# A second buffer for the gate blocks of layer two, a first stage with one chain of norms and its modulation a tile ahead, and five buffers for the samples' states

## The chip, the cores and the metric

The kernel runs on one core of a Trainium2 chip. The metric is the time of one execution on the device in microseconds (µs), the median of several runs. The core's engines are named as in the profile: PE multiplies matrices (PEld is its loading of weights), DVE works on vectors, ACT computes activations and copies, POOL is GpSimd, and SP issues the transfers (DMA) in order. Every transfer named here is issued on SP.

## What is computed

One step of a decoder with two layers, for a prompt of 1024 tokens and 8 samples of 4 tokens each (32 rows). Each layer shifts and scales the normed input by values that come from a condition vector, runs a token mixer, and adds the gated result to its input:

```
def modulate(x, c, norm_g, w_mod, b_mod):
    shift, scale, gate = jnp.split(jax.nn.silu(c) @ w_mod + b_mod, 3, axis=-1)
    h = rms_norm(x, norm_g) * (1 + scale[:, None]) + shift[:, None]
    return h, gate[:, None]

x <- x + gate(c) * Branch(RMSNorm(x) * (1 + scale(c)) + shift(c))
```

The mixer of layer one is attention in a sliding window of 128 positions (16 query heads, 4 key and value heads, learned sinks). The mixer of layer two is a gated DeltaNet: 8 query and key heads, 16 value heads of 128, a short convolution, and one state of 128 x 128 for each value head. The samples bring their own states: 8 samples of 16 heads, 8 MB in fp32, read and written once. In both layers the input projection also gives a SiLU gate path `z`, which multiplies the mixer's output ahead of the output projection. The width of the model is 1024.

## The kernel before

**Precision.** A large projection is three matmuls on split operands: high part by high part, low by high and high by low (`hhi`, `hlo` for the activations; `wh`, `wl` for the weights). The split of a piece of weights is a cast on ACT (`wh`) and a subtraction on DVE or POOL (`wl`).

**Order.** The order of instructions is fixed when the program is built. The class `Core` keeps a clock for each engine and adds up an estimated duration for each instruction; jobs (generators) yield conditions such as `ready`, `idle` and `soon`, and the planner takes up the one whose condition holds. Nearly every instruction passes through its wrapper, so the profile gives it the line L84; one tells them apart by the names of their tiles. The compute engines keep this order. Transfers are put in an order of their own on SP when the program is built, as their buffers come free there; on the chip SP issues them one after the other, and an issue that waits holds up those behind it.

**The first stage** makes `hhi` and `hlo`, the modulated input, and computes the first two column blocks of the input projection at the same time.

- `turn_x` transposes nine pieces of `x` on PE, and DVE copies them to `zo`; ACT sums the squares (`xss`).
- `scale_x(n0, n1)` turns the sums into 1/rms (`rsx`) by a chain of 12 small operations on DVE. It is called for pieces 0 to 4 after the fifth `turn_x`, and for pieces 5 to 8 at the end.
- `spread_x(gi)` spreads `rsx` over the partitions by matmuls, and ACT copies the result to `rsb`, for three groups of columns. For the samples POOL then makes `fs`.
- `modulate(e)` multiplies the condition by the modulation's weights for feature tile `e` (16 small matmuls on `wm`), and ACT copies the result to `ma`. `fold(e, ma)` adds up its rows by two matmuls, and DVE makes the scale `Sc` and the shift `Sh`.
- `shape_h(k)` makes feature tile `k` of `hhi` and `hlo`: DVE computes `fu` from `zo`, `Sc` and `rsb`, ACT adds the shift and rounds (`hhi`), and DVE takes the rest (`hlo`). For the 32 sample rows, four small operations do the same on POOL.
- `first_part(k, p)` adds feature tile `k` to column block `p`: nine matmuls into three banks of PSUM (`pj`, `pj`, `tr` for block 0, `lg`, `lg`, `ob` for block 1).

The loop over the eight tiles has, in this order, `fold(k+1)`, `shape_h(k+1)`, both parts of `first_part(k)`, and `modulate(k+2)`. After it, `kproj(0)` and `qproj(0,0)` evacuate the six banks, and `qproj(0,1)` runs its projection (matmuls at L537) into the banks that the ring `pj3` gives (`pj`, `pj`, `tr`).

**Layer two.** Its chunks of the prompt go through projection, convolution, the solution of a triangular system (`X`, `Xd`, `UZ`) and the recurrence (`us`, `vo`, `S`). For each finished pair of chunks, `gating` normalises `vo` and multiplies it by the gate: the block `zl` (128 x 512, 256 KB) is loaded from `zd`, where the gate path was stored; ACT scales `vo`; PE transposes it into `ps_tr`; DVE multiplies into `zl`; and `zl` is stored in `gTd`, from where the output projection reads it (`of`):

```
zl = gp.tile([P, 2, 2 * P], F32, tag="zl", name="zl", bufs=ZB)
nc.sync.dma_start(zl, zd[rs_, ts_].rearrange("(h p) i -> p h i", p=P))
...
nc.vector.scalar_tensor_tensor(zf, pt, ong, zf, ALU.mult, ALU.mult)
give("tr", pt)
nc.sync.dma_start(gTd[rs_, ts_].rearrange("(h p) i -> p h i", p=P), zl)
```

There are 32 such blocks, and `zl` has `ZB` = 1 buffer.

**The samples' states.** From about 1400 µs on, `states_times` loads the states in 32 units of 256 KB (`S<-in_states`) into a ring of `SB` = 4 buffers. It multiplies them in pairs (`ps_lg<-S,zq`) and, after each pair, loads two more. The planner puts these matmuls between those of the output projection. Later `new_states` loads the states again, updates them and writes them.

Of the kernel before, what the change touches and what calls it, by code (L numbers as in the profile page):

```python
# [9 lines left out]
ALU = mybir.AluOpType  # L10
# [4 lines left out]
P = 128  # L15
# [171 lines left out]
def f(ap):  # L187
    return ap.bitcast(F32)
# [26 lines left out]
def body(tc, I, O, cst_ap, dbg=None):  # L215
# [10 lines left out]
    ps = tc.tile_pool(name="ps", bufs=1, space=PSUM)  # L226
    ps_guard, ps = ps, ps.__enter__()
    banks = {"pj": 2, "tr": 1, "mi": 2, "ob": 1, "lg": 2}
    rings = {"pj3": ("pj", "pj", "tr"), "ch": ("mi", "mi", "ob")}
    turns = dict.fromkeys(rings, 0)  # L230
    any_bank, pj_tag = "mi", "pj3"

    nkeep = COFF["wmask"][0]
    ZB, VB, SB = 1, 3, 4
    SP = (5, 21)
    AM = (6, 9)
    K = {'split': 4, 'add': 3, 'attend': 12, 'turning': 14, 'modulate': 31, 'cached': 9, 'wo': 39, 'turn': 0, 'ahead': 2, 'taps': 2, 'gating': 5, 'decay': 27, 'samples': 9, 'load': 4, 'mod': 9, 'shape': 9, 'decays': 8, 'prepare': 0, 'gather': 30, 'finish': 55, 'states': 21, 'core': 4, 'new': 9}
# [9 lines left out]
    SE = ("vector", "vector", "vector", "vector")  # L247
    LB_, SL = TB
    XB, FB = 14, 3

    def psb(tag=None):
        tag = tag or any_bank
        if tag in rings:
            turns[tag] += 1
            tag = rings[tag][(turns[tag] - 1) % len(rings[tag])]
        t = ps.tile([P, 512], F32, tag=tag, name="ps_" + tag, bufs=banks[tag])
        return nc.slot(tag, banks[tag], t) if isinstance(nc, Core) else t
# [161 lines left out]
    def split_w(raw, alloc=None):  # L419
        nk, ncol = raw.shape[1:]  # L420
        if alloc is None:
            hi = wq.tile([P, nk, ncol], F32R, tag="wh", name="wh", bufs=3)
            lo = wq.tile([P, nk, ncol], F32R, tag="wl", name="wl", bufs=3)
        else:
            hi, lo = alloc()
        last_split[:] = [nc.scalar.copy(hi, raw)]
        nc.gpsimd.tensor_sub(lo, raw, f(hi))
        return hi, lo
# [188 lines left out]
    def scale_x(n0, n1):  # L617

        sv = sm.tile([P, n1 - n0], F32, tag="sv4", name="sv4")
        nc.vector.tensor_scalar(sv, xss[:, n0:n1], 1.0 / D, EPS, ALU.mult, ALU.add)  # L620
        rsqrt(nc, sm, rsx[:, n0:n1], sv, n1 - n0, tag=f"rx{n0}")

    def spread_x(gi):

        a, b = GRP[gi]
        pb = psb(("lg", "ob", "lg")[gi])
        for t in range(3 * gi, 3 * gi + 3):
            parts, n = P if t < NB else TS, turns_x.index(t)
            nc.tensor.matmul(pb[:, t * P - a:t * P - a + parts], rsx[0:parts, n:n + 1].to_broadcast([parts, P]),
                             ident[0:parts, 0:parts], start=True, stop=True)  # L630
        nc.scalar.copy(rsb[:, a:b], pb[:, 0:b - a])
        if gi == 2:
            for i in range(2):
                nc.gpsimd.tensor_tensor(fs[:, 4 * i:4 * i + 4], zo[i][:, :, TP:T],
                                        rsb[:, TP:T].unsqueeze(1).to_broadcast([P, 4, TS]), ALU.mult)

    def modulate(e):

        pm = psb("mi")[:, 0:256]
        for k in range(KD):  # L640
            q = k % 4
            nc.tensor.matmul(pm[32 * q:32 * q + 32, :], cT[:, k, :], wms[e, k // 4][:, q, :], start=(k < 4), stop=(k >= 4),
                             skip_group_check=True)
        ma = xp.tile([P, 256], F32, tag="ma", name="ma", bufs=2)
        nc.scalar.copy(ma, pm)
        return ma

    def fold(e, ma):

        mT = psb("mi")  # L650
        for c in range(2):
            nc.tensor.matmul(mT[:, 32 * c:32 * c + 32], ma[:, c * P:(c + 1) * P], C["fold32"], start=True, stop=True)
        nc.vector.tensor_scalar(Sc[0][:, e, :], mT[:, 32:41], bS[:, e:e + 1], gT[:, 0, e:e + 1], ALU.add, ALU.mult)
        nc.vector.tensor_scalar(Sh[0][:, e, :], mT[:, 0:9], bT[:, e:e + 1], None, ALU.add)

    def shape_h(k):

        u = xp.tile([P, TP], F32, tag="fu", name="fu", bufs=FB)
        sc, sh = Sc[0][:, k, 0:1], Sh[0][:, k, 0:1]
        spans = [slice(0, GW), slice(GW, TP)]  # L660
        for cs in spans:
            nc.vector.scalar_tensor_tensor(u[:, cs], zo[k // 4][:, k % 4, cs], sc, rsb[:, cs], ALU.mult, ALU.mult)
            nc.scalar.activation(hhi[:, k, cs], u[:, cs], AF.Identity, bias=sh)
        for cs in spans:
            nc.vector.scalar_tensor_tensor(hlo[:, k, cs], u[:, cs], sh, f(hhi[:, k, cs]), ALU.add, ALU.subtract)
        bc, f4 = [P, DB, DS], fs[:, k, :].rearrange("p (b t) -> p b t", t=DS)
        nc.gpsimd.tensor_tensor(f4, f4, Sc[0][:, k, 1:9].unsqueeze(2).to_broadcast(bc), ALU.mult)
        nc.gpsimd.tensor_tensor(f4, f4, Sh[0][:, k, 1:9].unsqueeze(2).to_broadcast(bc), ALU.add)
        nc.gpsimd.tensor_copy(hhi[:, k, TP:T], fs[:, k, :])
        nc.gpsimd.tensor_sub(hlo[:, k, TP:T], fs[:, k, :], f(hhi[:, k, TP:T]))  # L670

    fps, fraws, fws = [], {}, {}

    def first_load(q):
        fraws[q] = wp.tile([P, 4, P], F32, tag="wr", name="wr", bufs=4)
        queued(fraws[q], I["win01"][q])

    def first_part(k, p_):

        hi, lo = fws[k // 2]  # L680
        for gi, (a, b) in enumerate(GRP):
            for n, (x, y) in enumerate(((hi, hhi), (hi, hlo), (lo, hhi))):
                nc.tensor.matmul(fps[p_][gi], x[:, 2 * p_ + k % 2, :], y[:, k, a:b], start=(k == 0 and n == 0),
                                 stop=(k == KD - 1 and n == 2))
# [4 lines left out]
    for n, t in enumerate(turns_x):  # L689
        turn_x(n, t)  # L690
        if n == 1:
            modulation_rows()
        if n == 4:
            scale_x(0, 5)
    queued(cst[:, early:], cst_ap[:, early:nkeep])
    wmod_load(2)
    first_load(1)
    spread_x(0)
    scale_x(5, 9)
    ma = modulate(0)  # L700
    fws[0] = split_w(fraws.pop(0))
    spread_x(1)
    spread_x(2)
    fold(0, ma)
    shape_h(0)
    ma = modulate(1)
    fps += [[psb(tag)[:, 0:b - a] for (a, b), tag in zip(GRP, tags)] for tags in (("pj", "pj", "tr"), ("lg", "lg", "ob"))]
    wmod_load(3)
    for k in range(KD):
        if k + 1 < KD:  # L710
            fold(k + 1, ma)
            shape_h(k + 1)
        first_part(k, 0)
        if k % 2 == 0 and k + 2 < KD:
            fws[k // 2 + 1] = split_w(fraws.pop(k // 2 + 1))
        first_part(k, 1)
        if k + 2 < KD:
            ma = modulate(k + 2)
        if k + 4 < KD:
            wmod_load(k + 4)  # L720
            if k % 2 == 0:
                first_load(k // 2 + 2)
    raws = []
    for q in range(2):
        raws.append(wp.tile([P, 4, P], F32, tag="wr", name="wr", bufs=4))
# [15 lines left out]
    if True:  # L741
# [107 lines left out]
        spare_ = []  # L849

        def qproj(pr, g):
            qs = []

            def evac(gi, a0, b0, pj):
                if gi == 0 and pr == 0 and g > 1:

                    if g == 2:
                        spare_.append(zp.tile([P, 4, T], F32R, tag="zo1", name="zq"))
                    qs.extend(spare_[0][:, 2 * (g % 2) + a, :] for a in range(2))
                elif gi == 0:  # L860
                    for a in range(2):
                        m = 4 * pr + 2 * (g % 4) + a if pr else 2 * g + a
                        if m > 4:
                            until(lambda: begun[0] >= NB * (1 if m < 9 else 3))
                        qs.append(at.tile([P, T], F32R, tag="qs", name="qs", bufs=5))
                for a in range(2):
                    own = slice(64 * a, 64 * a + 64)
                    oth = slice(64 - 64 * a, 128 - 64 * a)
                    nc.scalar.activation(qs[a][own, a0:b0], pj[own], AF.Copy, scale=0.125)
                    nc.vector.scalar_tensor_tensor(qs[a][oth, a0:b0], pj[own], 0.125, f(qs[a][own, a0:b0]),  # L870
                                                   ALU.mult, ALU.subtract)
                    if gi == 2:
                        src = pj[own, 1024 - a0:1056 - a0].rearrange("p (b r t) -> p b r t", r=2, t=DS)
                        for r in range(2):
                            c0 = 48 * r + 4 * g
                            nc.scalar.activation(qz[:, 2 * pr + a, :, c0:c0 + 4], src[:, :, r, :], AF.Copy, scale=0.125)

            if pr == 0 and g == 0:
                for gi, (a, b) in enumerate(GRP):
                    with tc.issue_after(last_split[0].ins):  # L880
                        evac(gi, a, b, fps[1][gi])
            elif pr == 0 and g == 1:
                project(None, None, P, hhi, hlo, evac, wq01)
            else:
                projected(evac)
            return qs
# [1826 lines left out]
```

## Time and profile before

| what | value |
|---|---|
| median of the runs | 1701.39 µs (1697.44 to 1703.25) |
| profiled execution | 1698.41 µs |
| its span | 1696.6 µs |
| busy share of the span | PE 94%, PEld 84%, DVE 72%, ACT 50%, POOL 14% |
| read and written in HBM | 147.54 MB and 49.84 MB |

The span runs from the first to the last recorded instruction. All places in the trace are given as µs from its start. The column PEclk of the windows is the granted clock of PE as a share of its full rate. A timeline row gives the start, the duration, the engine, the instruction as out<-in, and in brackets the idle time of the engine ahead of it and what ended it.

### The profile page before, as it was taken

What the parts mean: (1) busy time and instruction counts of PE and PEld (TensorE: products, weight loads), DVE (VectorE), ACT (ScalarE), POOL (GpSimd) and SP (SyncE); (2) the same over time, 40 slices, a digit from 0 to 9 for tenths busy, and PEclk for the clock granted to TensorE, in tenths of its full rate; (3) what the DMA queues carried; (4) which work ended last, traced back from release to release, by engine and by line L of the source; (5) the groups of instructions that cost most, each with busy time, mean ns of one, the idle gap of its engine ahead of it and who ended that gap; (6) DMA issues with size and microseconds to landing.
All of it is one profiled execution on the core that took longest, in us unless ns stands there. A gap on an engine that the chain in (4) does not pass through costs nothing.

```text
span 1696.6 us, 30465 instructions
## 1 busy us (share of the span) xinstructions
PE 1602.7 (94%) x10544; PEld 1419.6 (84%) x10544; DVE 1218.4 (72%) x3797; ACT 845.1 (50%) x2414; POOL 237.6 (14%) x321
## 2 busy tenths in 40 slices
PE   7899999999999999989999899999999998888897
PEld 6798888988678999879999898999999986556675
DVE  5626677566665687878988788887888867267677
ACT  4526565444334664546654654646655654233332
POOL 2400000002222001020011101001010032132332
PEclk8999999999999999989999999999999999998999
DMA  9332211125242323133313224232242156773785
GB/s 347 108 128 93 75 53 51 57 60 155 86 146 91 119 61 101 52 85 89 116 51 99 78 69 116 67 106 77 67 126 58 54 174 177 225 230 112 249 262 168
DMA packets 190890, 196.79 MB, mean 116 GB/s; under 512 B 86432, under 2 KB 137472, under 8 KB 190688
## 3 DMA queue, kind: packets, MB, share of 16 engines
q1 hardware_dynamic: 190736, 194.84, 37.4%
q8 instruction: 83, 1.36, 0.3%
q14 instruction: 71, 0.58, 0.1%
HBM read 147.54 MB, written 49.84 MB: 116 GB/s over the span
## 4 chain that ended last, share of the span: by engine, by line
PE 43%; DVE 9%; DMA 9%; ACT 3%; issue 2%; SPq 1%; POOL 0%; POOLq 0%; DVEq 0%; ACTq 0%
PE ps_pj L84 27%; PE ps_lg L84 6%; PE ps_mi L84 5%; PE ps_ob L84 2%; PE ps_tr L84 2%; DMA gTd<-zl 2%; DMA S<-in_states 1%; DMA zl<-zd 1%; DMA of<-gTd 1%; DMA out_new_s_s<-S 1%; DVE zl L84 1%; DMA wr<-in_gdn_w_out 1%; DMA out_y_p<-xt 1%; DVE S L84 1%; DVE rst L84 1%
## 5 line engine op out<-in xcount | busy, mean ns | idle before, releaser
L84 PE MATMUL ps_pj<-h2lo,wh 128*128 128x384 f32 (+1 forms) x1128 | 380.4, 337 | 0.0
L84 PE MATMUL ps_pj<-h2hi,wl 128*128 128x384 f32 (+1 forms) x1128 | 378.9, 336 | 0.9 <-DVE wl L84 0.9
L84 PE MATMUL ps_pj<-h2hi,wh 128*128 128x384 f32 (+1 forms) x1128 | 379.4, 336 | 0.0
L84 PEld LDWEIGHTS ps_pj<-h2hi,wl 128*128 128x128 f32 x1128 | 213.9, 190 | 4.2 <-DVE wl L84 1.3
L84 PEld LDWEIGHTS ps_pj<-h2hi,wh 128*128 128x128 f32 x1128 | 214.2, 190 | 2.9
L84 PEld LDWEIGHTS ps_pj<-h2lo,wh 128*128 128x128 f32 x1128 | 214.0, 190 | 2.8
L84 POOL TENSOR_TENSOR Xd<-Xc,cst 32x128 f32<-32x128 f32 x128 | 68.5, 535 | 435.0 <-DMA Xc<-Xdd 251.5
L84 PE MATMUL ps_pj<-hlo,wh 128*128 128x384 f32 (+1 forms) x376 | 124.7, 332 | 0.0
L84 PE MATMUL ps_pj<-hhi,wh 128*128 128x384 f32 (+1 forms) x376 | 124.7, 332 | 0.0
L84 PE MATMUL ps_pj<-hhi,wl 128*128 128x384 f32 (+1 forms) x376 | 123.6, 329 | 0.0
L84 POOL TENSOR_TENSOR xt<-xt,y 128x512 f32<-128x512 f32 (+1 forms) x48 | 65.4, 1364 | 219.3 <-DVE y L84 186.4
L84 DVE TENSOR_TENSOR wl<-wr,wh 128x512 fp32r<-128x512 f32 x120 | 83.3, 694 | 15.5 <-ACT wh L84 15.1
L84 DVE SCALAR_TENSOR_TENSOR vT<-XR,cT,vT 128x384 f32<-128x384 f32 (+1 forms) x144 | 80.8, 572 | 9.9 <-ACT vT L84 9.2
L84 ACT CAST wh<-wr 128x512 fp32r<-128x512 f32 x128 | 78.6, 616 | 16.9 <-PE ps_pj L84 15.2
L84 PEld LDWEIGHTS ps_pj<-hlo,wh 128*128 128x128 f32 x376 | 71.0, 189 | 10.6 <-issue 10.2
L84 PEld LDWEIGHTS ps_pj<-hhi,wh 128*128 128x128 f32 x376 | 71.0, 189 | 4.0 <-issue 3.8
L84 PEld LDWEIGHTS ps_pj<-hhi,wl 128*128 128x128 f32 x376 | 71.0, 189 | 2.8 <-issue 2.7
L84 ACT ACTIVATE qe<-ps_mi,Eg 128x128 f32<-128x128 f32 x112 | 34.9, 363 | 70.8 <-PE ps_mi L84 68.9
L84 DVE TENSOR_TENSOR X<-X,tmp 128x126 f32<-128x126 f32 (+22 forms) x248 | 63.8, 257 | 8.5
L84 ACT COPY XR<-ps_pj 128x384 f32<-128x384 f32 (+1 forms) x96 | 43.3, 451 | 52.6 <-PE ps_pj L84 52.4
L84 DVE TENSOR_TENSOR tmp<-X 128x126 f32<-128x126 f32 (+22 forms) x248 | 62.3, 251 | 7.3 <-POOL X L84 3.4
L84 ACT ACTIVATE prob<-prob,nm 128x256 f32<-128x256 f32 (+1 forms) x128 | 62.2, 488 | 9.6 <-DVE nm L84 9.4
(540 smaller groups left out, 3933.9 us busy)
## 6 DMA issues: line engine op xcount, KB each, us to landing
wr<-in_gwb SPq DMA_DIRECT2D x96, 256.0 KB
S<-in_states SPq DMA_DIRECT2D x40, 256.0 KB
xt<-in_x_prompt SPq DMA_DIRECT2D x16, 512.0 KB
wm<-in_wm SPq DMA_DIRECT2D x16, 512.0 KB
wr<-in_winb SPq DMA_DIRECT2D x32, 256.0 KB
wmod<-in_w_mod SPq DMA_DIRECT2D x32, 256.0 KB
wm<-in_w_mod SPq DMA_DIRECT2D x32, 256.0 KB
DP<-gcr SPq DMA_DIRECT2D x64, 128.0 KB
```

Of the source, the lines that this page charges most:

```text
L84: inst = fn(*args, **kwargs)
```

## The change

It has three parts.

1. `ZB` goes from 1 to 2 (the ring of `zl`), and `SB` from 4 to 5 (the ring of the samples' states).
2. The first stage is put in another order. There is one call `scale_x(0, 9)` after all pieces of `x`; `modulate(0)` stands ahead of it, `modulate(1)` and `fold(0)` behind it and ahead of the three `spread_x`; `fold(1)` follows `shape_h(0)`. In the loop, `modulate(k+2)` stands between the two parts of `first_part(k)`. The samples' four operations of `shape_h` move from POOL to DVE (three) and ACT (one). `hold(n)` issues `n` matmuls whose result nobody reads: one ahead of the `spread_x` and three behind `fold(1)`. With `LATEP` False, the last three parts keep their old order.
3. A ring `next` = (`mi`, `mi`, `pj`) gives the banks for the projection in `qproj(0,1)`.

```
-    rings = {"pj3": ("pj", "pj", "tr"), "ch": ("mi", "mi", "ob")}
+    rings = {"pj3": ("pj", "pj", "tr"), "next": ("mi", "mi", "pj"), "ch": ("mi", "mi", "ob")}
...
-    ZB, VB, SB = 1, 3, 4
+    ZB, VB, SB = 2, 3, 5
...
+    FH, LATEP = (1, 3), False
...
+        bc, f4 = [P, DB, DS], fs[:, k, :].rearrange("p (b t) -> p b t", t=DS)
+        nc.vector.tensor_tensor(f4, f4, Sc[0][:, k, 1:9].unsqueeze(2).to_broadcast(bc), ALU.mult)
+        nc.vector.tensor_tensor(f4, f4, Sh[0][:, k, 1:9].unsqueeze(2).to_broadcast(bc), ALU.add)
+        nc.scalar.copy(hhi[:, k, TP:T], fs[:, k, :])
         for cs in spans:
             nc.vector.scalar_tensor_tensor(hlo[:, k, cs], u[:, cs], sh, f(hhi[:, k, cs]), ALU.add, ALU.subtract)
-        bc, f4 = [P, DB, DS], fs[:, k, :].rearrange("p (b t) -> p b t", t=DS)
-        nc.gpsimd.tensor_tensor(f4, f4, Sc[0][:, k, 1:9].unsqueeze(2).to_broadcast(bc), ALU.mult)
-        nc.gpsimd.tensor_tensor(f4, f4, Sh[0][:, k, 1:9].unsqueeze(2).to_broadcast(bc), ALU.add)
-        nc.gpsimd.tensor_copy(hhi[:, k, TP:T], fs[:, k, :])
-        nc.gpsimd.tensor_sub(hlo[:, k, TP:T], fs[:, k, :], f(hhi[:, k, TP:T]))
+        nc.vector.tensor_sub(hlo[:, k, TP:T], fs[:, k, :], f(hhi[:, k, TP:T]))
+
+    def hold(n):
+
+        pt = psb("mi")
+        for _ in range(n):
+            nc.tensor.matmul(pt[:, 0:384], ident, zo[0][:, 0, 0:384], start=True, stop=True)
...
-        if n == 4:
-            scale_x(0, 5)
...
-    spread_x(0)
-    scale_x(5, 9)
     ma = modulate(0)
+    scale_x(0, 9)
+    ma1 = modulate(1)
+    fold(0, ma)
     fws[0] = split_w(fraws.pop(0))
-    spread_x(1)
-    spread_x(2)
-    fold(0, ma)
+    hold(FH[0])
+    for gi in range(3):
+        spread_x(gi)
     shape_h(0)
-    ma = modulate(1)
+    fold(1, ma1)
+    hold(FH[1])
...
         if k + 1 < KD:
-            fold(k + 1, ma)
+            if k:
+                fold(k + 1, ma)
             shape_h(k + 1)
-        first_part(k, 0)
+        if k < KD - 1:
+            first_part(k, 0)
         if k % 2 == 0 and k + 2 < KD:
             fws[k // 2 + 1] = split_w(fraws.pop(k // 2 + 1))
-        first_part(k, 1)
         if k + 2 < KD:
             ma = modulate(k + 2)
+        if k < KD - 2:
+            first_part(k, 1)
...
+    for k, p_ in ((KD - 1, 0), (KD - 2, 1), (KD - 1, 1)) if LATEP else ((KD - 2, 1), (KD - 1, 0), (KD - 1, 1)):
+        first_part(k, p_)
...
             elif pr == 0 and g == 1:
+                pj_tag = "next"
                 project(None, None, P, hhi, hlo, evac, wq01)
+                pj_tag = "pj3"
```

Apart from the first stage, the compute engines keep the order of their instructions up to about 1420 µs. Behind that the planner puts the matmuls on `S` at other places among those of the output projection.

More of the change, by code (lines that the diff above doesn't have):

```diff
@@ L851, in qproj @@
         def qproj(pr, g):
+            nonlocal pj_tag
             qs = []
```

## The prediction

> **What bounds the kernel now.** I read the page first, then the waits, then the windows over stretches that differ, and the timelines of the stretches that stood out. Ahead of all, the page's parts 1, 2 and 4:
>
> ```profile
> span 1696.6 us, 30465 instructions
> PE 1602.7 (94%) x10544; PEld 1419.6 (84%) x10544; DVE 1218.4 (72%) x3797; ACT 845.1 (50%) x2414; POOL 237.6 (14%) x321
> ...
> PE 43%; DVE 9%; DMA 9%; ACT 3%; issue 2%; SPq 1%; POOL 0%; POOLq 0%; DVEq 0%; ACTq 0%
> ```
>
> PE is the bound: 94 µs of the span are without PE work, and no edit here removes a product of weights. So a gain can only be PE's idle time and the stretches in which its clock is half. The waits (engine, tile, releaser: total µs, times, longest) say which idle time the change touches:
>
> ```profile
> DVE zl L84 <- DMA zl<-zd: 25.2, 11, 7.4
> PE ps_tr L84 <- DVE zl L84: 9.7, 6, 4.3
> PEld ps_mi L84 <- ACT ma L84: 8.3, 7, 2.2
> PE ps_lg L84 <- DMA S<-in_states: 8.2, 5, 3.3
> ```
>
> Three places follow: the first stage (`ma`), the gate blocks (`zl`) and the samples' states (`S`). The windows give each one's ceiling (stretch, length, busy time of PE, PEld, DVE, ACT, POOL, granted clock, DMA share, GB/s):
>
> ```profile
> 25.00:30.00 5.00, 5.00 (x30) 3.76 (x30) 1.31 (x4) 1.06 (x3) 1.60 (x5) 0.50 1.03 408
> 30.00:35.00 5.00, 3.71 (x20) 3.25 (x13) 4.14 (x8) 2.43 (x5) 2.70 (x6) 0.50 1.02 404
> ...
> 40.00:75.00 35.00, 29.55 (x230) 24.94 (x229) 23.12 (x45) 17.49 (x32) 16.90 (x28) 1.00 0.16 42
> 75.00:90.00 15.00, 15.00 (x85) 13.95 (x86) 8.03 (x16) 9.87 (x28) 7.60 (x6) 0.89 0.71 247
> ...
> 560.00:700.00 140.00, 138.89 (x987) 135.45 (x985) 109.88 (x351) 77.58 (x205) 9.12 (x24) 1.00 0.32 88
> 700.00:750.00 50.00, 41.99 (x246) 38.49 (x244) 36.86 (x120) 27.85 (x93) 6.90 (x13) 0.90 0.28 75
> ...
> 950.00:1000.00 50.00, 44.53 (x275) 41.80 (x274) 37.25 (x112) 30.23 (x81) 0.26 (x3) 0.93 0.26 72
> ...
> 1250.00:1300.00 50.00, 47.54 (x367) 45.87 (x365) 42.01 (x121) 33.26 (x88) 10.07 (x16) 0.97 0.31 81
> ...
> 1400.00:1450.00 50.00, 40.79 (x186) 31.78 (x186) 36.95 (x98) 23.28 (x75) 14.71 (x18) 0.93 0.66 177
> 1450.00:1500.00 50.00, 44.99 (x245) 26.53 (x246) 11.13 (x22) 7.16 (x15) 8.42 (x7) 0.93 0.82 248
> ```
>
> Where nothing disturbs it (560 to 700) PE is idle 1%. A window at clock 0.90 lost another 5.0 µs of PE's full rate.
>
> **The first stage.** On PE, from the last transposes of `x` to the first matmul of `first_part` (`rsx` the norms' factors, `wm` the modulation's weights, `ma` its folded rows, `zo,cst` the dummies), before:
>
> ```order
> L84 MATMUL ps_lg<-cst,rsx 128x128 x3
> L84 MATMUL ps_mi<-wm_122,cT 32x256 x4
> L84 MATMUL ps_mi<-wm_124,cT 32x256 x4
> L84 MATMUL ps_ob<-cst,rsx 128x128 x3
> L84 MATMUL ps_lg<-cst,rsx 128x128 x2
> L84 MATMUL ps_lg<-cst,rsx 128x32
> L84 MATMUL ps_mi<-cst,ma 128x32 x2
> L84 MATMUL ps_mi<-wm_128,cT 32x256 x4
> L84 MATMUL ps_mi<-wm_130,cT 32x256 x4
> L84 MATMUL ps_mi<-cst,ma 128x32 x2
> L84 MATMUL ps_pj<-hhi,wh 128x384
> ```
>
> and after:
>
> ```order
> L84 MATMUL ps_mi<-wm_122,cT 32x256 x4
> L84 MATMUL ps_mi<-wm_124,cT 32x256 x4
> L84 MATMUL ps_mi<-wm_128,cT 32x256 x4
> L84 MATMUL ps_mi<-wm_130,cT 32x256 x4
> L84 MATMUL ps_mi<-cst,ma 128x32 x2
> L84 MATMUL ps_mi<-zo,cst 128x384
> L84 MATMUL ps_lg<-cst,rsx 128x128 x3
> L84 MATMUL ps_ob<-cst,rsx 128x128 x3
> L84 MATMUL ps_lg<-cst,rsx 128x128 x2
> L84 MATMUL ps_lg<-cst,rsx 128x32
> L84 MATMUL ps_mi<-cst,ma 128x32 x2
> L84 MATMUL ps_mi<-zo,cst 128x384 x3
> ```
>
> Both modulations and the first fold now run while DVE works on the norms, and nothing but a fold and three dummies stands between the spread and `first_part`. The timelines of PE, DVE and POOL price it (start, duration, instruction, idle time before it and its releaser):
>
> ```profile
> 22.24 1.26 POOL L84 TENSOR_TENSOR wl<-wr,wh 128x512 fp32r<-128x512 f32 x1 [12.71 <-ACT wh L84]
> ...
> 14.44 0.16 DVE L84 TENSOR_SCALAR sv<-xss 128x5 f32<-128x5 f32 x1
> 16.73 0.69 DVE L84 COPY zo<-ps_tr 128x512 f32<-128x512 f32 x1
> 21.52 0.16 DVE L84 TENSOR_SCALAR sv<-xss 128x4 f32<-128x4 f32 x1
> 22.32 1.20 DVE L84 SCALAR_TENSOR_TENSOR rst<-rst,sv 128x4 f32<-128x4 f32 x1
> 28.89 0.22 DVE L84 TENSOR_SCALAR Sh<-ps_mi,gb 128x9 f32<-128x9 f32 x1
> 29.09 1.48 DVE L84 SCALAR_TENSOR_TENSOR fu<-zo,Sc,rsb 128x384 f32<-128x384 f32 x2
> ...
> 24.96 1.22 PE L84 MATMUL ps_ob<-cst,rsx 128*128 128x128 f32 x4 [2.81 <-DVE rsx L84]
> 28.52 1.94 PE L84 MATMUL ps_mi<-wm,cT 128*32 128x256 f32 x16
> 32.62 0.67 PE L84 MATMUL ps_pj<-hhi,wh 128*128 128x384 f32 x1
> 39.69 0.63 PE L84 MATMUL ps_mi<-cst,ma 128*128 128x32 f32 x4 [0.55 <-ACT ma L84]
> 40.16 0.42 PE L84 MATMUL ps_pj<-hhi,wh 128*128 128x384 f32 x1
> 60.81 0.42 PE L84 MATMUL ps_pj<-hhi,wh 128*128 128x384 f32 x1
> 65.99 0.42 PE L84 MATMUL ps_pj<-hhi,wh 128*128 128x384 f32 x1
> 75.00 0.41 PE L537 MATMUL ps_pj<-hhi,wh 128*128 128x384 f32 x1 [2.67 <-DVE kll L806]
> ```
>
> *Front.* The first chain of norms takes 14.44 to 16.73 in the midst of DVE's copies; without it the copies end 2.3 earlier and the single chain ends near 21.7, not 24.9. The spread follows 3 µs earlier, and `fu` comes straight behind it, not behind a fold at 28.7: `fu` at about 24.5 (was 29.09), first matmul at about 27.5 (was 32.62): 5.0. PE runs in order, so a late `wm` of the second tile would now hold the spread behind it; DMA is full (1.03 at 25 to 30) and the row at 28.52 only says that it had landed by then. At worst that takes all 5.0; I take nothing for it and leave it to the lower bound.
> *First tile.* From 32.62 to 40.16 it takes 7.54, most of it at clock 0.50; a warm one is 65.99 − 60.81 = 5.18. With the wait for `ma` gone it is 4.63, so 2.9 if PE is warm by then, near 0 if it is cold as now.
> *The other six tiles.* `modulate` stands ahead of 9 matmuls instead of behind them, which covers the 0.55 of `ma`: 6 × 0.55 = 3.3. The samples' operations add 24 on DVE; by the row of `Sh`, 0.22 each, that is 5.3 µs over 8 tiles, under DVE's 12 idle of 35 (third window).
> *Its end.* `qproj(0,1)` starts in the two banks `mi`, no longer behind `kproj`'s evacuation: 2.67, and 11% of the window from 75 to 90, 1.7, for the half clock that follows the idle time. The next users of `mi`, the turns of `kx`, then wait for an evacuation of this projection; I take 1.9, by bounds of 0 and the 2.67 it replaces.
> Sum 5.0 + 2.9 + 3.3 + 4.4 − 1.9 = 13.7. Half of the cold first tile stays likely, so I take **12**; bounds 6 and 14. The dummies, each shorter than the cold 0.67 at 32.62, run in idle time.
>
> The Trainium skill ("TensorE: Matmul & The Clock Gate", Part 1: The HAM clock gate) has PE at half clock after an idle window of about 3.4 µs in a free-running count, so that four dummies need not suffice; by it the first tile would be warm or cold by chance, and the term 10 or 14. The windows at 0.50 agree with the half clock.
>
> **The gate blocks.** On SP, one pair of gate blocks in the second layer (`zl` the block, `gTd` where it is stored, `zd` where it is from), before:
>
> ```order
> L84 DMA gTd_5982<-zl_13180 128x2x256
> L84 DMA wr_13494<-in_gwb 128x512
> L84 DMA zl_13267<-zd_5981 128x2x256
> L84 DMA DP_13485<-gcr_5979 128x256 x2
> L84 DMA zd_5981<-th_13328 128x384
> L84 DMA gTd_5982<-zl_13267 128x2x256
> L84 DMA zl_13549<-zd_5981 128x2x256
> ```
>
> and after:
>
> ```order
> L84 DMA gTd_5973<-zl_13171 128x2x256
> L84 DMA wr_13485<-in_gwb 128x512
> L84 DMA zl_13540<-zd_5972 128x2x256
> L84 DMA DP_13476<-gcr_5970 128x256 x2
> L84 DMA gTd_5973<-zl_13258 128x2x256
> L84 DMA zd_5972<-th_13319 128x384
> L84 DMA zl_13614<-zd_5972 128x2x256
> ```
>
> The load stands at the same place, behind the same store, but it now brings the block after the next: the pair's second block (13267 before, 13258 after) is in SBUF a block ahead. What the old order cost (the chain's steps first, then DVE and PE):
>
> ```profile
> 717.47 3.33 DMA gTd<-zl
> 720.87 2.70 DMA zl<-zd
> ...
> 723.64 0.75 DVE L84 SCALAR_TENSOR_TENSOR zl<-ps_tr,ong,zl 128x512 f32<-128x512 f32 x1 [2.90 <-DMA zl<-zd]
> ...
> 724.54 0.66 PE L84 MATMUL ps_tr<-cst,vT 128*128 128x128 f32 x2 [4.34 <-DVE zl L84]
> 731.51 1.22 PE L84 MATMUL ps_mi<-us,ktok 128*128 128x256 f32 x2 [2.18 <-DVE us L84]
> 963.88 0.87 PE L84 MATMUL ps_tr<-cst,vT 128*128 128x128 f32 x3 [3.98 <-DVE zl L84]
> ...
> 1429.37 0.70 PE L84 MATMUL ps_mi<-us,ktok 128*128 128x256 f32 x2 [2.41 <-DVE us L84]
> 1450.09 0.63 PE L84 MATMUL ps_lg<-S,zq 128*32 128x256 f32 x4 [3.28 <-DMA S<-in_states]
> ```
>
> Store, then load, 6.0 µs in a row, with DVE and then PE waiting behind. SP itself still waits for the store's landing (3.33) with the next store behind it, as before; that delays `gTd`, which is read much later. Ceiling by the windows: at 700, 950 and 1250 PE is idle 8.0 + 5.5 + 2.5 = 16.0, less 1% of 150, and the clocks 0.90, 0.93 and 0.97 are 5.0 + 3.5 + 1.5 = 10.0 more: 24.5. Floor: the two longest PE stalls with `zl` as releaser, 4.34 + 3.98, of which DVE's queue (36.86 busy of 50) may take half back: 4. I take two thirds of the ceiling, **16**, since the stalls lie at the start of each cold stretch and vanish whole.
>
> **The states.** With five buffers the loads of `S` are issued one sooner; PE's matmuls on `S` stand 2 to 12 output matmuls earlier in its order. PE waits 8.2 for `S`; at 1450 to 1500 it runs at 0.93 and the transfers at 248 GB/s, where 408 went at 25. Of 8.2 + 3.5 I take 4, and for the stall of 2.41 at 1429, which follows a late `zl` too, 2 more: **6**; bounds −4 (earlier matmuls meet later loads) and 12.
>
> **Sum.** 12 + 16 + 6 = 34 from the profiled execution's 1698.4 gives 1664.4. The median of the runs, 1701.4, is 3.0 above that execution, so the forecast is **1667**.
>
> **Rivals.**
> (a) *The first stage gains half.* The row at 22.32 is a DVE operation of 0.17 stretched to 1.20 while POOL computed `wl` (22.24, 1.26); two more DVE operations a tile can meet it. Eight such meetings of about 1.0, or a cold first tile, leave 5 of 12: 1674. For: DVE feeds the tile; against: POOL has 35 operations fewer to meet. The Trainium skill ("SBUF — State Buffer", SBUF: two separate sides) calls the ports that DVE and GpSimd share an exclusive lock for the whole instruction, which speaks against moving these operations to DVE; the row agrees. Chance 0.12.
> (b) *The gate blocks give little*, 2 of 16: DVE's backlog at the chunk's end is the next to be late (`us`, 2.18 at 731.51). Against it: those waits follow DVE's own 2.90. 1681. Chance 0.13.
> (c) *Slower: PE waits for states.* Its 16 pairs of state matmuls stand in front of output matmuls that are ready. If the earlier place makes each wait as at 1450.09, that is 16 × 3.28 = 52 against a gain of 28: 1725. It decides from 1.8 a pair. Against: the loads also start earlier, and only 5 of them make PE wait now. Chance 0.03.
> (d) *All is recovered*: 14 + 24.5 + 12 = 50: 1651. Chance 0.10.
> (e) *The second buffer isn't used*, because the scheduler keeps the order: the rows above speak against it; 12 + 6 leaves 1683. Chance 0.02.
>
> **How the numbers follow.** The forecast, 0.60, spans 1658 to 1676. The range takes in (a), (b) and (d): 1650 to 1686. A measurement of this kernel tells about 0.3% (5 µs) from no change. All cases but (c) lie below 1696, so faster 0.95; (c) gives slower 0.03; 0.02 remains for a mixture within 0.3%.
>
> **What would show it.** Right: the first matmul of `first_part` near 27.5 and seven tiles of about 4.65 behind it; no 2.67 ahead of L537's matmul; DVE's wait for `zl<-zd` below 5 of 25.2, and a clock of 1.00 in the 50 µs that answer to 700 and 950, some 12 to 20 earlier; PE's wait for `S` at 4. Wrong: `S` waits above 20, tiles above 5.2 with DVE as releaser, or PE stalls behind `us` where those behind `zl` were.

## The result, and the profile after

The changed kernel took 1671.66 µs in the median of 4 runs (1669.56 to 1675.52), the kernel before 1699.45 in 4 runs beside it (the 1701.39 given ahead of the prediction is the median of the first 3 of them). The ratio is 0.9836, with a 95% interval of 0.9807 to 0.9866. The forecast was 1667, the range 1650 to 1686. The profiled execution took 1669.87; its page, parts 1, 2 (the granted clock in tenths over 40 slices) and 4:

```profile
span 1668.1 us, 30471 instructions
PE 1594.5 (96%) x10552; PEld 1411.4 (85%) x10552; DVE 1224.1 (73%) x3809; ACT 844.8 (51%) x2422; POOL 221.8 (13%) x289
...
PEclk9999999999999999999999999999999999998998
...
PE 49%; DVE 8%; DMA 4%; ACT 3%; issue 1%; POOL 0%; SPq 0%; POOLq 0%; ACTq 0%; DVEq 0%
```

PE's idle time fell from 94 to 74 µs and DMA's share of the chain from 9% to 4%. PE was busy for 8 µs less with four matmuls more, which fits the clock: matmuls that ran at half clock now run at the whole one. The waits that answer to those shown of before (µs, times, longest):

```profile
PEld ps_lg L84 <- DMA S<-in_states: 9.8, 10, 2.9
PE ps_lg L84 <- DMA S<-in_states: 5.2, 5, 2.5
PE ps_tr L84 <- DVE zl L84: 3.3, 5, 1.4
```

DVE's wait for `zl<-zd`, 25.2 before, no longer occurs. The windows of the same work (columns as before):

```profile
25.00:30.00 5.00, 5.00 (x28) 4.12 (x26) 2.46 (x5) 2.53 (x5) 1.45 (x2) 0.86 1.04 410
30.00:35.00 5.00, 4.92 (x37) 3.37 (x35) 4.92 (x12) 2.62 (x7) 0.46 (x1) 1.00 1.02 406
35.00:65.00 30.00, 29.55 (x233) 25.43 (x233) 26.44 (x58) 14.85 (x32) 6.24 (x5) 1.00 0.27 89
...
685.00:735.00 50.00, 44.34 (x295) 40.61 (x294) 42.04 (x136) 30.60 (x99) 7.18 (x14) 1.00 0.30 78
...
935.00:985.00 50.00, 46.99 (x306) 44.19 (x305) 41.18 (x128) 32.88 (x93) 0.26 (x3) 1.00 0.27 80
...
1235.00:1285.00 50.00, 49.82 (x400) 47.52 (x399) 44.22 (x119) 32.85 (x84) 9.91 (x19) 1.00 0.34 90
...
1430.00:1480.00 50.00, 47.20 (x253) 28.19 (x251) 18.53 (x42) 13.12 (x22) 10.32 (x8) 1.00 0.82 251
```

The clock is whole where it was 0.90, 0.93 and 0.97, and PE's idle time in those three is 5.7, 3.0 and 0.2 (8.0, 5.5 and 2.5 before). Where the gain arose is best seen from the start of one and the same instruction in both profiled executions:

| instruction | before | after | gained so far |
|---|---|---|---|
| DVE's first `nm<-mx,nsk`, at the head of attention | 120.59 | 109.36 | 11.2 |
| DVE's first `zl`, in layer two | 716.44 | 706.54 | 9.9 |
| DVE's 28th `zl`, ahead of the output projection | 1373.97 | 1348.10 | 25.9 |
| DVE's `KQT`, behind the states' matmuls | 1525.24 | 1495.76 | 29.5 |
| end of the span | 1696.6 | 1668.1 | 28.5 |

### The profile page after: what moved, and what is told of

Read it like the earlier page. It is cut to its first block, busy times and chain, and to the rows that moved or that the text cites. A ratio compares the mean times of both kernels' runs of the same rounds, so it can differ in the third digit from the quotient of the medians.

```text
span 1668.1 us, 30471 instructions
## 1 busy us (share of the span) xinstructions
PE 1594.5 (96%) x10552; PEld 1411.4 (85%) x10552; DVE 1224.1 (73%) x3809; ACT 844.8 (51%) x2422; POOL 221.8 (13%) x289
## 3 DMA queue, kind: packets, MB, share of 16 engines
q8 instruction: 84, 1.38, 0.3%
## 4 chain that ended last, share of the span: by engine, by line
PE 49%; DVE 8%; DMA 4%; ACT 3%; issue 1%; POOL 0%; SPq 0%; POOLq 0%; ACTq 0%; DVEq 0%
PE ps_pj L84 31%; PE ps_lg L84 7%; PE ps_mi L84 6%; PE ps_ob L84 3%; PE ps_tr L84 3%; DMA S<-in_states 1%; DMA of<-gTd 1%; DVE rst L84 1%; DVE y L84 1%; DVE S L84 1%; DVE rsw L84 0%; ACT L84 0%; DVE oH L84 0%; ACT jc L84 0%; DMA xt<-x2d 0%
## 5 line engine op out<-in xcount | busy, mean ns | idle before, releaser
L84 PEld LDWEIGHTS ps_pj<-hlo,wh 128*128 128x128 f32 x376 | 70.7, 188 | 11.2 <-issue 10.2
```

Of the source, the lines that this page charges most:

```text
L84: inst = fn(*args, **kwargs)
```

## The experiments

All ratios are to the kernel before, run beside it on the same chip. The experiments ran on three chips; ratios are compared, and the starts of instructions in the traces. The fifth experiment, the changed kernel once more, is the mark; it ran on the chip of the three that follow it. One execution of each kernel was traced, two of the changed kernel.

**One gate buffer.** The changed kernel with one edit; the compute engines keep its order.

```diff
-    ZB, VB, SB = 2, 3, 5
+    ZB, VB, SB = 1, 3, 5
```

> The changed kernel with one gate buffer again. Compute engines keep the order of the changed kernel, only SP differs. Theory 1 (the load a block ahead removes stalls of DVE and PE at the pairs of gate blocks): 14 us from 700 to 1400 come back and 2 to 5 more in the tail, 1686 to 1691; DVE waits for zl<-zd by about 25 again and the clock falls to half near 710 and 945. Rival (the earlier start of layer two moved the pairs clear of other work, the buffer itself matters little): below 1676, without those waits.

1693.42 (before: 1702.41), ratio 0.9949 (0.9930 to 0.9969). The waits of DVE and of PE are back:

```profile
DVE zl L84 <- DMA zl<-zd: 26.1, 11, 8.7
PE ps_tr L84 <- DVE zl L84: 9.4, 6, 4.3
```

So is the half clock near 715 and 954. Between DVE's first and 28th `zl` lie 656.9 µs, 657.5 before and 641.6 in the changed kernel: 15 µs come back there, and 4 more between that and `KQT` (151.7 against 147.7). Theory 1 holds. An earlier start alone does nothing for these stalls.

**Only the second gate buffer.** The kernel before with one edit.

```diff
-    ZB, VB, SB = 1, 3, 4
+    ZB, VB, SB = 2, 3, 4
```

> The kernel before with two gate buffers and nothing else; PE keeps its old order. Theory 1: 14 to 18 us below before, 1682 to 1686, and the start of layer two at its old time. Rival (the gain needs the five state buffers or the new first stage as well): 0 to 6 us.

1684.29, ratio 0.9891 (0.9868 to 0.9914): 18.6 µs by the ratio, 18.1 by the medians. First to 28th `zl`: 641.9. The buffer does this by itself.

**Four state buffers.**

```diff
-    ZB, VB, SB = 2, 3, 5
+    ZB, VB, SB = 2, 3, 4
```

> The changed kernel with four state buffers. Theory 2 (the fifth buffer takes about half of PE's waits for S away): PE waits 8 for S instead of 5.2, 3 to 4 us slower, 1675. Rival (what the tail gained came from the gate blocks alone): within 1 us of the changed kernel, 1671 to 1673.

1673.13, ratio 0.9839 (0.9811 to 0.9866): the time doesn't tell it from the changed kernel. Its waits:

```profile
PEld ps_lg L84 <- DMA S<-in_states: 12.1, 11, 3.4
PE ps_lg L84 <- DMA S<-in_states: 7.5, 4, 2.9
```

PE waits 7.5 for the states, 5.2 in the first trace of the changed kernel and 6.8 in the mark's. The 28th `zl` to `KQT` takes 149.2 against 147.7 and 147.6. These differences are no larger than those between traces of other kernels with five state buffers; what speaks for the buffer is all traces together. PE waits 3.7 to 7.0 in the ten with five state buffers, 7.5 to 9.3 in the four with four. From the 28th `zl` to `KQT` it takes 144.9 to 149.3 in the nine with two gate and five state buffers, 149.2 and 150.9 in the two with two and four. So the fifth buffer shortens these waits, by 2.8 µs in the mean of the traces; whether any of it reaches the end is open.

**The old banks.**

```diff
             elif pr == 0 and g == 1:
-                pj_tag = "next"
+                pj_tag = "pj3"
```

> The changed kernel with the old banks for the second query projection. Theory 3 (the ring is worth the wait of 2.67 and the half clock behind it, less the 1.68 that the turns of kx now wait): 2 to 3 us slower, 1674, and an idle time of about 2.7 on PE ahead of the projection. Rival (the wait only moves): within 1 us, 1671 to 1673.

1674.28, ratio 0.9828 (0.9804 to 0.9851), again no difference that the time can tell. In the timeline of PE the wait is back, where the changed kernel had the smaller one at the turns of `kx` (first row: old banks, second: the changed kernel, from the fence after it):

```profile
67.93 0.66 PE L538 MATMUL ps_pj<-hhi,wh 128*128 128x384 f32 x1 [3.07 <-DVE kll L818]
```

```profile
75.88 0.30 PE L826 MATMUL ps_mi<-cst,kx 128*128 128x128 f32 x1 [1.68 <-DVE qs L883]
```

From the first matmul of `first_part` to the first `nm` it takes 82.5 µs, not 79.6: the ring is worth 2.9 in the first stage. The 2.9 is smaller than the scatter of the total.

**The mark.** The changed kernel, unedited.

> The changed kernel once more, beside the next three on the same chip, as the mark to compare them with: a ratio of 0.981 to 0.987 to before. The first matmul of first_part moved between 29.7 and 31.5 in the runs so far, as the second tile's modulation waits for its weights; it should again lie there.

1674.74 (before: 1702.28), ratio 0.9850 (0.9827 to 0.9873). The first matmul of `first_part` starts at 29.79, within what was expected.

**The samples' operations on POOL.**

```diff
-        nc.vector.tensor_tensor(f4, f4, Sc[0][:, k, 1:9].unsqueeze(2).to_broadcast(bc), ALU.mult)
-        nc.vector.tensor_tensor(f4, f4, Sh[0][:, k, 1:9].unsqueeze(2).to_broadcast(bc), ALU.add)
-        nc.scalar.copy(hhi[:, k, TP:T], fs[:, k, :])
...
-        nc.vector.tensor_sub(hlo[:, k, TP:T], fs[:, k, :], f(hhi[:, k, TP:T]))
+        nc.gpsimd.tensor_tensor(f4, f4, Sc[0][:, k, 1:9].unsqueeze(2).to_broadcast(bc), ALU.mult)
+        nc.gpsimd.tensor_tensor(f4, f4, Sh[0][:, k, 1:9].unsqueeze(2).to_broadcast(bc), ALU.add)
+        nc.gpsimd.tensor_copy(hhi[:, k, TP:T], fs[:, k, :])
+        nc.gpsimd.tensor_sub(hlo[:, k, TP:T], fs[:, k, :], f(hhi[:, k, TP:T]))
```

> The changed kernel with the samples' four operations of each tile on POOL again. Theory (PE sets the tile's 4.53, DVE has room either way): tiles stay at 4.5 to 4.6, total within 1 us of the changed kernel. Rival (a) of the prediction (DVE's extra operations meet POOL's wl and eat gain): DVE's work in the loop falls, the wait of 0.45 at the last tile goes and 1 to 5 us are won. Third: POOL's chain of 2.2 us ends later than hlo did, PE waits for it in the groups of the samples' columns, 1 to 4 us slower.

1674.35, ratio 0.9839 (0.9815 to 0.9864), not told from the mark. What rival (a) had foreseen is in the trace of the changed kernel, POOL's timeline first, then DVE's:

```profile
43.32 1.38 POOL L84 TENSOR_TENSOR wl<-wr,wh 128x512 fp32r<-128x512 f32 x1 [7.40 <-ACT wh L84]
```

```profile
43.45 1.29 DVE L84 TENSOR_TENSOR hlo<-fs,hhi 128x32 fp32r<-128x32 f32 x1
48.09 0.18 DVE L84 TENSOR_TENSOR hlo<-fs,hhi 128x32 fp32r<-128x32 f32 x1
52.50 1.29 DVE L84 TENSOR_TENSOR hlo<-fs,hhi 128x32 fp32r<-128x32 f32 x1
```

An operation of 0.18 takes 1.29 when POOL computes `wl` beside it. Nearly all of it is hidden: PE sets the tile, and only at the last tile it waits, 0.45 for `hlo`. With the operations on POOL that wait is gone and the way from `first_part` to `nm` is 78.5, not 79.6. In this execution the first `nm` came 3.8 earlier than in the mark; the rest of that is the earlier first matmul (27.14 against 29.79), where the clock happened to be whole and the weights came about 1 µs earlier.

**No dummies.**

```diff
-    FH, LATEP = (1, 3), False
+    FH, LATEP = (0, 0), False
```

> The changed kernel without the four dummy matmuls. Theory (they keep PE's windows busy, so that the clock is whole when first_part starts): the granted clock stays at 0.5 into the first tile, which takes 6 to 7.5 instead of about 5, 1.5 to 3.5 us slower. Rival (the spread and the modulations keep PE busy enough; the dummies cost a little): clock the same, first matmul up to 1 us earlier, total 0 to 1 us faster.

1673.88, ratio 0.9831 (0.9806 to 0.9856). The windows without the dummies:

```profile
27.00:30.00 3.00, 1.18 (x5) 0.82 (x5) 2.76 (x5) 1.62 (x4) 1.45 (x2) 0.88 1.03 408
30.00:33.00 3.00, 3.00 (x20) 2.39 (x23) 2.92 (x10) 1.53 (x4) 0.00 (x0) 0.55 1.03 408
```

and with them, in the changed kernel:

```profile
27.00:30.00 3.00, 3.00 (x16) 2.12 (x15) 1.92 (x5) 1.96 (x4) 1.45 (x2) 1.00 1.03 404
30.00:33.00 3.00, 2.92 (x26) 1.66 (x24) 3.00 (x8) 0.89 (x3) 0.00 (x0) 1.00 1.02 406
```

The clock behaves as the theory said, 0.55 at 30 to 33 without them. The price it named is not paid: without the dummy ahead of it the spread starts at 23.01, not 24.42, and the first matmul at 27.73. PE then waits 1.38 for DVE's `hlo` and runs at half clock, and the fold of the third tile stands at 34.95 against 34.81 in the mark. In these executions the dummies neither gain nor cost.

**`modulate` behind both parts.**

```diff
-        if k + 2 < KD:
-            ma = modulate(k + 2)
         if k < KD - 2:
             first_part(k, 1)
+        if k + 2 < KD:
+            ma = modulate(k + 2)
```

> The changed kernel with modulate(k+2) behind both parts again. Theory (its place covers the wait for ma): the wait of 0.55 returns in 5 or 6 tiles, 2.8 to 3.3 us slower, tiles near 5.1. Rival (DVE's chain is what ends last in a tile, as it is busy for 26.4 of 30): tiles at 4.6 to 4.8, 0 to 1.5 us.

1679.64, ratio 0.9871 (0.9848 to 0.9894), 4.9 above the mark by the medians, though the intervals overlap. Its PE shows the old wait in each tile, two of the six rows:

```profile
36.08 0.63 PE L84 MATMUL ps_mi<-cst,ma 128*128 128x32 f32 x4 [0.55 <-ACT ma L84]
41.25 0.63 PE L84 MATMUL ps_mi<-cst,ma 128*128 128x32 f32 x4 [0.55 <-ACT ma L84]
```

The tile is 5.17 again, 4.54 in the changed kernel, and from `first_part` to `nm` it takes 83.5 instead of 79.6: 3.9, a little above what was expected.

**The first stage alone.** The changed kernel with the old numbers of buffers.

```diff
-    ZB, VB, SB = 2, 3, 5
+    ZB, VB, SB = 1, 3, 4
```

> The kernel before with the new first stage and the new ring of banks, one gate buffer and four state buffers. Theory (the parts add up): 10 to 11 us below before, nearly all of it gained ahead of vproj. Rival (an earlier layer one gives time back later): under 7 us.

1696.78 in 12 runs (before: 1702.75 in 17), ratio 0.9970 (0.9949 to 0.9991): 5 µs by the ratio, 6 by the medians, with an interval of about 1.5 to 9, not 10 to 11. The first `nm` is 8.9 earlier than before (the first matmul came late, at 32.88, with the clock at half up to 32), the first `zl` 7.2, the 28th 5.0, and `KQT` no longer at all. The windows where most of that went:

```profile
1390.00:1410.00 20.00, 14.47 (x55) 10.40 (x54) 10.20 (x25) 10.20 (x33) 4.60 (x4) 0.74 0.88 233
1440.00:1470.00 30.00, 23.72 (x118) 13.75 (x117) 6.93 (x18) 4.38 (x14) 3.82 (x3) 0.83 0.82 225
1480.00:1492.00 12.00, 9.17 (x41) 4.52 (x40) 0.69 (x1) 0.00 (x0) 1.28 (x1) 0.72 0.70 212
```

and the same work before:

```profile
1396.00:1416.00 20.00, 15.05 (x64) 11.24 (x63) 12.66 (x34) 10.93 (x34) 5.13 (x4) 0.91 0.82 224
1446.00:1476.00 30.00, 24.14 (x121) 15.23 (x121) 6.53 (x15) 3.78 (x11) 4.92 (x4) 0.89 0.77 218
1482.00:1494.00 12.00, 9.67 (x58) 4.80 (x58) 1.87 (x4) 0.62 (x1) 1.78 (x2) 1.00 0.81 261
```

PE is idle for 14.6 µs in these and for 13.1 before; the clock differs more, 0.74, 0.83 and 0.72 against 0.91, 0.89 and 1.00. Times 20, 30 and 12 µs that is 8.6 µs of PE's full rate, more than the 5.1 that were lost from the 28th `zl` to `KQT`. The rival is right for the total. In the profiled execution the half clock is the likeliest cause of the loss in that stretch; the 3.9 lost ahead of it aren't explained, and that the same happens in the median of the 12 isn't shown, since only one was traced.

**`modulate(1)` behind the spread.**

```diff
-    FH, LATEP = (1, 3), False
+    FH, LATEP = (4, 0), False
...
-    ma1 = modulate(1)
     fold(0, ma)
     fws[0] = split_w(fraws.pop(0))
     hold(FH[0])
     for gi in range(3):
         spread_x(gi)
+    ma1 = modulate(1)
     shape_h(0)
     fold(1, ma1)
```

> The changed kernel with modulate(1) behind the three spreads, where it takes the place of the three dummies, and all four dummies ahead of the spreads. Theory (the second tile's late weights hold the spread in PE's order): the spread starts at 22.6 to 22.9 with rsx, not 24.4, the first matmul of first_part about 1.5 us earlier, 1 to 2 us faster than the changed kernel. Rival (the matmuls of fold(1), still ahead of first_part, only move the wait: ma comes behind hhi or rsb on ACT): first matmul within 0.5 us, total within 1 us.

1671.13 (before: 1702.75), ratio 0.9819 (0.9790 to 0.9848). The spread on PE, in this kernel and then in the changed one:

```profile
23.04 0.83 PE L84 MATMUL ps_lg<-cst,rsx 128*128 128x128 f32 x6
```

```profile
20.57 0.64 PE L84 MATMUL ps_mi<-wm,cT 128*32 128x256 f32 x8 [0.80 <-DMA wm<-in_wm]
21.85 0.64 PE L84 MATMUL ps_mi<-wm,cT 128*32 128x256 f32 x8 [0.64 <-DMA wm<-in_wm]
24.42 1.49 PE L84 MATMUL ps_lg<-cst,rsx 128*128 128x128 f32 x6
29.78 0.63 PE L84 MATMUL ps_pj<-hhi,wh 128*128 128x384 f32 x1
```

The spread starts 1.4 earlier, the first matmul 2.5 earlier (27.32) and the first `nm` 2.3 earlier (107.05). What the order itself does is seen against the end of the norms. DVE's last row of their chain, in the changed kernel, in this one and in the next one below:

```profile
22.49 0.17 DVE L84 SCALAR_TENSOR_TENSOR rsx<-rst,rsw 128x9 f32<-128x9 f32 x1
```

```profile
22.64 0.17 DVE L84 SCALAR_TENSOR_TENSOR rsx<-rst,rsw 128x9 f32<-128x9 f32 x1
```

```profile
20.04 0.17 DVE L84 SCALAR_TENSOR_TENSOR rsx<-rst,rsw 128x9 f32<-128x9 f32 x1
```

In the changed kernel the spread starts 1.8 behind the norms' end, since the late weights, a fold and a dummy stand ahead of it; in the ten traces with `modulate(1)` ahead of the spread it is 1.2 to 3.4 behind. Here it starts 0.2 behind, so the theory holds for the order. In the next kernel, with the same order and earlier norms, it starts 2.5 behind (22.66): there the four dummies hold it. And the 2.3 µs are not shown to be the price of the order: the kernel with the samples on POOL keeps `modulate(1)` in its place and has its first matmul at 27.14 and its first `nm` at 105.61, after norms that ended at 20.88 and with a whole clock. The total's interval overlaps the mark's.

**The same, and the samples on POOL.** Both edits of the kernels above.

```diff
+    ma1 = modulate(1)
     shape_h(0)
...
+        nc.gpsimd.tensor_tensor(f4, f4, Sc[0][:, k, 1:9].unsqueeze(2).to_broadcast(bc), ALU.mult)
```

> The same, and the samples' four operations on POOL. Theory: both gains add up, vproj starts 2 to 4 us earlier than in the changed kernel, ratio to before 0.981 to 0.983. Rival: later half-clock windows scatter by more than that from run to run and the total can't tell it from the changed kernel.

1669.70, ratio 0.9809 (0.9777 to 0.9841). The first `nm` is at 107.17, 2.2 ahead of the mark's but no better than with the first edit alone: this execution had the clock at half from 29 to 32. The rival was right that the total can't tell this kernel from the changed one; whether both gains add up stays open.

**The weights first, and the samples on POOL.** Beside the operations on POOL:

```diff
     wmod_load(0)
-    first_load(0)
     wmod_load(1)
+    first_load(0)
```

> The changed kernel with the samples' operations on POOL and the second tile's modulation weights loaded ahead of the first piece of projection weights. Theory: they land about 0.65 earlier (256 KB at 400 GB/s), the waits of modulate(1) fall from 1.4 to below 0.8 and the first matmul comes about 0.6 earlier than in the kernel with only the operations on POOL. Rival: the split of the projection weights now comes late, no gain.

1668.96, ratio 0.9803 (0.9771 to 0.9834), the lowest of all, 0.5% below the mark with intervals that just overlap. It is the lowest of several and ran on another chip than the mark, so that it beats the changed kernel isn't shown. `modulate` waits 1.6 in all for its weights, 2.5 with the samples on POOL alone; the waits of `modulate(1)` are 1.3, not below 0.8. The spread stands only 1.2 behind the norms, but the first matmul (27.20 against 27.14) and the first `nm` (105.67 against 105.61) are no earlier: the load order gains nothing by itself here.

## Why the prediction was right

It was right in the direction, the range and the largest term. The gain was 28 µs where 34 was forecast: the states' term was too high, and a loss that no term held took 1.3. In the table, the forecast terms and what the starts of instructions in the profiled executions give.

| term | forecast | by the starts of instructions |
|---|---|---|
| first stage | 12 | 11.2 |
| from there to layer two | 0 | −1.3 |
| gate blocks | 16 | 16.0 |
| states and tail | 6 | 2.6 |
| sum | 34 | 28.5 |

**Gate blocks.** The reading of the order was right: the pair's second block lies ready. DVE's two rows of the pair, and SP's rows:

```profile
706.54 0.74 DVE L84 SCALAR_TENSOR_TENSOR zl<-ps_tr,ong,zl 128x512 f32<-128x512 f32 x1
710.76 0.74 DVE L84 SCALAR_TENSOR_TENSOR zl<-ps_tr,ong,zl 128x512 f32<-128x512 f32 x1
```

```profile
707.57 0.38 SPq L84 DMA_DIRECT2D gTd<-zl  x1
711.12 0.37 SPq L84 DMA_DIRECT2D zl<-zd  x1
711.58 0.42 SPq L84 DMA_DIRECT2D gTd<-zl  x1
```

The pair is 4.2 apart, 7.2 before. The next load still goes out only 3.5 behind the store's issue, when the store has landed, as foreseen, and the second store goes out behind it to no harm. What stayed is in PE's row:

```profile
711.65 0.41 PE L84 MATMUL ps_tr<-cst,vT 128*128 128x128 f32 x2 [1.36 <-DVE zl L84]
717.79 0.70 PE L84 MATMUL ps_mi<-us,ktok 128*128 128x256 f32 x2 [2.18 <-DVE us L84]
```

The 4.34 is now 1.36, and the 2.18 behind `us` is the same: it was not a late `zl` that caused it. Two thirds of the ceiling was a choice, and the reason given for it (stalls vanish whole) is true of DVE's wait but not of PE's. From the first to the 28th `zl`, before and after (columns as in the windows):

```profile
716.44:1373.97 657.53, 633.89 (x4506) 603.23 (x4505) 540.41 (x1704) 378.40 (x1155) 61.15 (x128) 0.98 0.31 87
```

```profile
706.54:1348.10 641.56, 627.47 (x4491) 599.25 (x4489) 541.00 (x1705) 377.87 (x1154) 60.17 (x126) 1.00 0.31 89
```

PE's idle time fell by 9.5 and its busy time by 6.4: the first is the stalls, the second fits the half clock that is gone. That the sum meets the 16 to the tenth is luck: the eleven traces with two gate buffers take 641.6 to 647.3 for this stretch, the three with one 656.9 to 659.8.

**First stage.** The front gave 2.8, not 5.0. The step that failed is the late `wm`, named and priced at nothing: `modulate(1)` waits 1.44 for its weights with the fold, a dummy and the spread behind it in PE's order, and the spread starts at 24.42, 1.8 behind the norms. So not all dummies ran in idle time, as the prediction had it. The clock is partly at half there, 0.67 at 22 to 25 and 0.77 at 25 to 28. The norms themselves ended at 22.7, not near 21.7: DVE's copies ended 1.3 earlier, not 2.3. How the 2.2 divide among these isn't shown. The first tile gave 2.1 of 2.9 (35.26 − 29.78 = 5.48). The six tiles gave 3.8 for 3.3, less 0.45 at the last. The ring gave 2.9 where 2.5 was taken. These parts make 11.2 of the 13.7 summed; that 12 lies so near is luck, as it was 13.7 cut for a cold first tile, while most of what fell short was the front. In the five traces with this first stage unedited the first `nm` is 8.9 to 11.2 earlier than before. The samples' operations cost DVE 5.9 + 1.7 + 1.5 = 9.1 µs by their groups, where 5.3 was taken by the row of `Sh`:

```profile
L84 DVE TENSOR_TENSOR hlo<-fs,hhi 128x32 fp32r<-128x32 f32 x8 | 5.9, 738 | 0.0
L84 DVE TENSOR_TENSOR fs<-fs,Sc 128x32 f32<-128x32 f32 x8 | 1.7, 214 | 0.0
L84 DVE TENSOR_TENSOR fs<-fs,Sh 128x32 f32<-128x32 f32 x8 | 1.5, 192 | 0.2
```

The difference comes from four meetings with POOL at 1.1 each, which is rival (a)'s mechanism. (POOL had 32 operations fewer, 289 against 321, not 35.) The Trainium skill ("SBUF — State Buffer", SBUF: two separate sides) has the loser of the shared ports blocked for the whole instruction; 1.29 instead of 0.18 beside a `wl` of 1.38 agrees. Rival (a) lost because PE, not DVE, ends last in a tile.

**Behind the first stage** 1.3 were lost that no term held. PE's last wait ahead of that stretch, at `ps_lg<-cst,gbs` (573.02 before, 561.88 after), still has 11.1 of the gain. So the loss lies in the stretch from there to the first `zl`, in which PE had no idle time over 0.2 in either execution. It takes 143.4 before and 144.1 with only the second gate buffer, but 144.4 to 144.8 in all twelve traces with the new first stage. So it comes with that stage and not by chance: over the first 600 matmuls the projection's stand 2 ns wider apart each, 0.9 in all, where the kernel with only the second gate buffer loses nothing. No row says why; this stays open.

**States.** PE's wait for `S` fell by 3.0, from 8.2 to 5.2 (6.8 in the mark), where 4 was taken together with the clock. The stall of 2.41 at 1429 is gone, and it did follow a late `zl`: it is 2.0 to 2.4 in the three traces with one gate buffer and absent in the eleven with two. But PE's wait for DVE's `vo` ahead of it is 2.51 where it was 0.67; it lies between 0.7 and 2.7 from trace to trace. From the 28th `zl` to `KQT` 3.6 were gained, and behind it 1.0 was lost again, which is less than the scatter of that last stretch (169.5 to 174.4 in the fourteen traces). The term was mis-sized: 2.6 for 6. Rival (c) had its place right but not its price; PE still waits for the states 5 times.

## What to carry to other kernels

Where a ring of one buffer is loaded behind its own store on an in-order queue, the page shows store and load one after the other in the chain; a second buffer takes the load a whole block ahead even if it keeps its place in the queue. On an in-order engine a step that is moved ahead of others carries its own late input with it: look where its weights land ahead of moving it. And cost the half clock that follows a stall beside the stall itself: here PE's busy time, which half clock stretches, fell by 8 of the 28.5 µs, the rest was idle time.

## What the runs showed that was not expected

**The scatter of a kernel goes with its clock.** Executions of one kernel on one chip differ by 11 µs and more, and the mean granted clock goes with the span: in the 12 runs of the first stage alone from 0.974 to 0.981 with spans from 1700.6 to 1689.3, 1.2 µs for each 0.001 (correlation −0.82). The whole 0.007 is about 11.9 µs of PE's full rate (0.007 × 1696). Which is the cause isn't shown, as stalls and half clock come together in these traces. From the kernel before (0.977, mean of 9 runs) to the mark beside it (0.985, mean of 4) it is 0.008, or some 14 µs of PE's full rate by the same reckoning. That is an upper estimate of the clock's share in the gain, since it counts time in which PE was idle; PE's busy time fell by 8.2.

**The same stall costs half clock in one execution and none in the next.** The windows around the first pair of gate blocks, in the changed kernel's two profiled executions, first and then the mark:

```profile
709.00:720.00 11.00, 6.81 (x37) 5.27 (x38) 9.19 (x37) 2.97 (x11) 0.00 (x0) 1.00 0.41 135
720.00:730.00 10.00, 10.00 (x65) 10.00 (x64) 6.76 (x21) 7.53 (x28) 3.70 (x7) 1.00 0.59 120
```

```profile
709.00:720.00 11.00, 6.43 (x31) 4.30 (x32) 10.08 (x40) 3.99 (x14) 0.00 (x0) 0.97 0.45 140
720.00:730.00 10.00, 10.00 (x52) 9.73 (x51) 4.49 (x19) 6.11 (x24) 2.27 (x4) 0.86 0.58 120
```

PE's stalls are the same to 0.02 µs in both (1.36 and 1.35, then 2.18 twice), 1.5 µs later in the second. In the first the clock stays whole, in the second it is at half for about 3.4 µs. The Trainium skill ("TensorE: Matmul & The Clock Gate", Part 1: The HAM clock gate) says that the window is free-running, so that its place against the work is chance; these rows agree. A gain of 1 to 3 µs can thus not be told from the totals of a few runs. The starts of the same instruction in two traces tell it where no half clock falls into the stretch (first matmul to first `nm`: 79.6 in four of the five traces with the same first stage). Where it does they scatter as well (28th `zl` to `KQT`: 144.9 to 149.3), and it takes several traces.
